# A hybrid encoder block on one core: the transfers that turn the feed-forward input spread over the projections, and a third of the weight sums moved to the last gates

## The chip, the cores and the metric

The kernel runs on one core of a Trainium2 chip. Its metric is the device time of one execution in microseconds (us). Three runs of the kernel before gave 865.10, 865.54 and 866.94 us, median 865.54. The profile is of one more execution, which took 866.11 us. Its trace covers a span of 864.3 us of that; the remaining 1.8 us lie around the span.

The engines have the profile's names: PE (TensorE, matrix products), DVE (VectorE), ACT (ScalarE), POOL (GpSimd), and SP (SyncE, which here only issues DMA transfers). POOL issues transfers too. Each engine works through its own instructions strictly in the order in which they stand. An instruction that waits for a semaphore holds up everything behind it on that engine.

## What is computed

The input is x of 512 rows by 1024 columns. Three token mixers (an mLSTM, a neighbourhood attention with a table of biases, a cross-attention into a memory) are merged by gates, projected, added to x, and followed by a feed-forward part and a normalization:

```python
h = rms_norm(x, mix_norm_g)
ml_q, ml_k, ml_v, ml_o, ml_gates, na_qkv, xa_q, merge_pre = split(h @ w_in)
g_ml, g_na, g_xa = split(sigmoid(merge_pre + b_merge_gate))
merged = g_ml * (y_ml @ w_br_ml) + g_na * (y_na @ w_br_na) + g_xa * (y_xa @ w_br_xa)
x = x + merged @ w_out
a, u = split(rms_norm(x, ffn_norm_g) @ w_ffn_up)          # 2816 columns each
x = x + (gelu(dwconv3(a, w_ffn_conv)) * u) @ w_ffn_down
return rms_norm(x, final_norm_g)
```

## The kernel before

**Layout and products.** Activations lie transposed, with channels on the 128 partitions and the 512 rows along the free axis, so x is eight tiles of 128x512. Each float32 product is made of three matmuls (`mm3`, L259 to L262): high part by high part, high part by low part, low part by high part. A *projection* (`proj`, L455) makes one tile of 128 output channels from eight input tiles, with 24 matmuls into one PSUM bank.

**Weights.** The weights are consumed in one fixed list of blocks (`BLOCKS`), each of 512 KB for a projection. SP loads a block into a tile `wr` (`emit_raw`, L206; three buffers, asked for three blocks ahead). It is then split in two halves: for each half ACT makes the high part `wh` (L242) and DVE the low part `wl` (L243, block minus high part). There are four buffers for high and four for low halves. In the code the split of a block stands one block ahead of the projection that uses it (`SPLIT_AHEAD`), but the instructions of each engine are put into their final order when the program is built, by a scheduler that may move them ahead of or behind their place in the code.

**Weight sums.** The down projection is computed from sums of quarters of its weight matrix, T1 to T4, held in DRAM. `sum_steps` (L163 to L174) makes them in 24 steps. Each step is a one-column copy on POOL (L169), which waits for the low half of a weight block and so sets the step's time, and behind it one transfer on POOL's own queue: a copy of a third of a quarter (L172) or the addition of another third to it (L174). The table `SUMS` (L64) says how many steps go to a projection of a kind: 0.5 is one step for every second projection. Before, 2 steps go to the `nak` projections, 6 to the first gates, 8 to the 8 output projections and 8 to the feed-forward projections `ua`.

**The stages around the change**, by the time in the profile's span:

- *Last gates* (about 383 to 436 us): eight gate projections of branch 2. Between them runs the end of the neighbourhood attention. Each of its steps loads a bias tile `nab` of 256 KB (`bias_tile`, L896, two buffers, on SP), and adds it to the scores on DVE (L914, two per step); ACT takes the exponentials (L919) and scales them (L922), and PE transposes the result (L928).
- *Output projections* (to about 510 us): eight projections `out` (loop at L1208), each followed by the addition of a residual tile that SP loads from `xT` (L1206, L1214) and a split of the new x2 into high and low parts.
- *Feed-forward, first half* (`hh` = 0, from about 510 us): the loop over f at L1344 takes two projections per step, `ua` and `uu`. On the `ua` bank follow, in a row: L518 (DVE, multiplies the bank into `pad`), L520 (ACT), L521 and L522 (DVE), which make the convolution, then L1375 (ACT), L1376 (DVE), L1377 (ACT) and L1378 (DVE), which make the gelu, and L1379 (POOL, a multiplication). On the `uu` bank: L1390 (DVE) multiplies it by the gelu, then come two halves of a split, L1322 (ACT) and L1323 (DVE), with a subtraction on POOL between them (L1393).
- From f = 1 to f = 8 each step also *turns* one tile of x2, since the final sum is wanted with rows on the partitions. `turned` (L557) does a transposition of 32x32 blocks on DVE (L559) and four transfers on SP (L561, one for each *band* of 32 partitions, 64 KB each in pieces of 128 bytes) to `c_d` in DRAM. At f = 9 `fetch` (L1237) reads `c_d` back with four transfers of 512 KB. `turn_keys` uses `turned` as well, much earlier in the program.

Of the kernel before, what the change touches and what calls it, by code (L numbers as in the profile page):

```python
# [11 lines left out]
F32 = mybir.dt.float32  # L12
# [5 lines left out]
P = 128  # L18
S = 512
D = 1024  # L20
KT = D // P
NT = S // P
# [38 lines left out]
NVEC = _o  # L61


SUMS = {"nak": 0.5, ("g", 0): 0.75, "out": 1.0, "ua": 0.75}  # L64
PRODUCTS = (("B11", "T3"), ("B21", "T1", "T2", "B22", "T4"))
QUARTERS = ("B11", "B12", "B21", "B22")

# [54 lines left out]
def hybrid_block(ctx, tc, xg, xT, memT, wflat, vecs, gbias, nabias, out):  # L122
    nc = tc.nc
    V, A, G, PE, SY = nc.vector, nc.scalar, nc.gpsimd, nc.tensor, nc.sync
# [5 lines left out]
    tp = ctx.enter_context(tc.tile_pool(name="tp", bufs=2))  # L130
    mmp = ctx.enter_context(tc.tile_pool(name="mmp", bufs=4, space=bass.MemoryType.PSUM))
    atp = ctx.enter_context(tc.tile_pool(name="atp", bufs=4, space=bass.MemoryType.PSUM))
    dp = ctx.enter_context(tc.tile_pool(name="dp", bufs=1, space=bass.MemoryType.DRAM))
# [3 lines left out]
    def nm(s):  # L137
        uid[0] += 1
        return f"{s}_{uid[0]}"

    def unit(dt=F32):
        return up.tile([P, UNIT], dt, tag="unit", name=nm("u"))
# [191 lines left out]
    for i in range(2):  # L334
        t = cp.tile([P, 514], F32, name=f"pad{i}")
# [119 lines left out]
    def proj(key, XHs, XLs, n=S, at={}, ps=None):  # L455

        ws = weights(key)
        if (key[0], key[1]) in SUMS or key[0] in SUMS:
            sum_step(SUMS.get(key[0]) or SUMS[key[:2]], ws)
        k0 = 0 if ps is None else 1  # L460
        if ps is None:
            ps = mmps()
        for k in range(k0, KT):
            mm3(ps[:, :n], ws[k][0], ws[k][1], XHs[k], XLs[k], k == 0, k == KT - 1)
            if k == 1:
                flush()
            if k in at:
                at[k]()
        return ps
# [60 lines left out]
    qT, kT = unit(), unit()  # L530
# [25 lines left out]

    def turned(x, src, dst, o=0):  # L557

        V.transpose(x, src)  # L559
        for a in range(4):  # L560
            SY.dma_start(dst[:, o + 32 * a:o + 32 * a + 32].rearrange("(b i) j -> i b j", i=32),  # L561
                         x[32 * a:32 * a + 32].rearrange("i (b j) -> i b j", j=32))

    kt_d = [dp.tile([S, P], F32, name=f"kt_d{f}") for f in range(4)]

    def turn_keys(f):

        with tc.issue_after(st["lo"]):
            turned(tp.tile([P, S], F32, tag="H", name=nm("kx"), bufs=4), kT[:, f * S:(f + 1) * S], kt_d[f])

    Gt = cp.tile([P, NT, 16], F32, name="Gt")
    va_u = unit()
# [3 lines left out]
    for c in range(3):  # L576
        n, nk = TMC[c], TMK[c]
# [142 lines left out]
    def ml_all():  # L720
# [18 lines left out]
        def keys(h):  # L739
# [4 lines left out]
            wva = u[:, :774].rearrange("p (d c e) -> p d c e", d=2, c=3)  # L744
            C = u[:, 774:1548].rearrange("p (d c e) -> p d c e", d=2, c=3)

# [47 lines left out]

        def values_J(h, J, E, ps, C, H, ss):
            js = slice(J * P, (J + 1) * P)
# [297 lines left out]
    for f in range(4):  # L1094
        ps = proj(("o", f), XH, XL)
        t = scr()
# [50 lines left out]
    for br in range(3):  # L1147
# [19 lines left out]
        for fp in range(4):  # L1167
# [9 lines left out]
            for i in range(2):  # L1177
                f = 2 * fp + i
# [18 lines left out]
    x2 = [x2u[f // 4][:, (f % 4) * S:(f % 4 + 1) * S] for f in range(KT)]  # L1197
# [2 lines left out]
    HL = [h2[k // 4 * 2 + 1][:, (k % 4) * S:(k % 4 + 1) * S] for k in range(KT)]  # L1200
    acc2 = cp.tile([P, S], F32, name="acc_2", tag="acc", bufs=1)
    xrs = {}

    def load_residual(f):
        xrs[f] = scr()
# [2 lines left out]
    for f in range(KT):  # L1208
        if f == 0:
            load_residual(0)  # L1210
        if f + 1 < KT:
            load_residual(f + 1)
        ps = proj(("out", f), GH, GL)
        V.tensor_tensor(x2[f], ps, xrs[f], op=ALU.add)  # L1214
        split_act(HH[f], HL[f], x2[f], vcol("ffn_g", f))
        if f == 0:
            A.activation(acc2, x2[f], AF.Square)
        else:
            sq = scr()
            A.activation(sq, x2[f], AF.Square)  # L1220
            V.scalar_tensor_tensor(acc2, acc2, EPS * D / P if f == 1 else 0.0, sq, op0=ALU.add, op1=ALU.add)


    C = [unit(), unit()]

    def cv(t, f):
        o = t % 2 * D + f * S
        return C[t // 2][:, o:o + S]

    c_d = dp.tile([S, D], F32, name="c_d")  # L1230

    def turn(f):

        turned(C[f // 4][:, (f % 4) * S:(f % 4 + 1) * S], x2[f], c_d, f * P)

    def fetch(t):
        SY.dma_start(C[t // 2][:, t % 2 * D:(t % 2 + 1) * D], c_d[t * P:(t + 1) * P, :])  # L1237
# [98 lines left out]
    for hh in range(2):  # L1336
        if hh == 0:
            a11, s3 = parts(), parts()
        else:
            ru = [unit() for _ in range(3)]  # L1340
            r1 = [ru[j // 4][:, j % 4 * S:(j % 4 + 1) * S] for j in range(HF)]
            a12, s1 = parts(), parts()
        for j in range(HF):
            f = HF * hh + j  # L1344
            if f == 0:
                wa, wu = weights(("ua", f)), weights(("uu", f))
                pa, pu = mmps(), mmps()
                for k in range(KT):
                    if k < KT - 1:
                        mm3(pa, wa[k][0], wa[k][1], HH[k], HL[k], k == 0, False)  # L1350
                for k in range(KT - 1):
                    mm3(pu, wu[k][0], wu[k][1], HH[k], HL[k], k == 0, False)
                k = KT - 1
                mm3(pa, wa[k][0], wa[k][1], HH[k], HL[k], False, True)
                rb2 = rstd_wide(square_sums(two_parts(acc2, S), S), S, "2")
                mm3(pu, wu[k][0], wu[k][1], HH[k], HL[k], False, True)
                pa1 = proj(("ua", 1), HH, HL)
                pu1 = proj(("uu", 1), HH, HL)
            else:
                pa = pa1 if f == 1 else proj(("ua", f), HH, HL)  # L1360
                if 1 <= f < KT + 1:
                    turn(f - 1)
                if f == KT + 1:
                    for t in range(NT):
                        fetch(t)
            cell = {}
            ve = V if j >= HF - 2 else G

            def conved(f=f, pa=pa, cell=cell):
                cell["c"] = conv(pa, rb2, "ffw", "ffb", f, FT)  # L1370

            def gelu(cell=cell, ve=ve):

                c, sq = cell["c"], scr()
                A.activation(sq, c, AF.Square)  # L1375
                V.scalar_tensor_tensor(sq, sq, GC, c, op0=ALU.add, op1=ALU.mult)  # L1376
                A.activation(sq, sq, AF.Tanh, scale=GK)  # L1377
                V.scalar_tensor_tensor(c, sq, 1.0, c, op0=ALU.add, op1=ALU.mult)  # L1378
                ve.tensor_tensor(c, c, rb2, op=ALU.mult)  # L1379

            if j < HF - 1:
                conved()
                gelu()
            if f > 0:
                pu = pu1 if f == 1 else proj(("uu", f), HH, HL)

            def gated(j=j, pu=pu, cell=cell, ve=ve):

                r, q, c = (r1 if hh else r0)[j], r0[j], cell["c"]
                V.scalar_tensor_tensor(r, pu, 0.5, c, op0=ALU.mult, op1=ALU.mult)  # L1390
                if hh == 0:
                    split_half(a11, j, r[:, one_])
                    ve.tensor_tensor(r[:, one_], r[:, two_], r[:, one_], op=ALU.subtract)  # L1393
                    late.append(lambda: split_half(s3, j, r[:, one_]))
                else:
                    split_half(a12, j, r[:, one_])
                    ve.tensor_tensor(q[:, two_], q[:, two_], r[:, two_], op=ALU.subtract)
                    late.append(lambda: split_half(s1, j, q[:, two_]))
                    ve.tensor_tensor(q[:, one_], q[:, one_], r[:, two_], op=ALU.subtract)
                    ve.tensor_tensor(r[:, one_], r[:, one_], q[:, one_], op=ALU.add)  # L1400

            if j < HF - 1:
                gated()
        if hh == 0:
            pa_, pd = [atps() for _ in range(2)], [mmps() for _ in range(2)]
            product("B11", a11, pa_, True, then={0: [conved], 1: [gelu], 2: [gated]})
            product("T3", s3, pd, True, then={1: [lambda: gather(pa_, 0, 0, ALU.add)]})
            late.append(lambda b=pd: (gather(b, 1, 0, ALU.subtract), gather(b, 1, 1, ALU.add)))
# [175 lines left out]
```

## Time and profile before

| quantity | value |
|---|---|
| runs: median (lowest to highest) | 865.54 us (865.10 to 866.94) |
| the profiled execution | 866.11 us |
| its span in the trace | 864.3 us |
| mean granted PE clock | 0.997 of full speed |
| DVE, ACT, POOL busy | 633.5, 476.1, 164.5 us |
| queue 1 (SP's transfers) | 107.66 MB, 38.7% of 16 DMA engines' time |
| queue 0 (POOL's transfers) | 29.39 MB, 14.0% |

The table is from the head of the profile's page. Busy time there is the time in which an engine has an instruction in work. For PE that includes waits inside its pipeline at half clock, so its share alone doesn't say that nothing is lost. The granted clock is the share of clock pulses that the throttle let through. The rows on PE itself are shown in the prediction.

### The profile page before, as it was taken

Reading aid. Unit: us, or ns where it says so; the run is one execution under the profiler, and the core shown is the slowest. Engines: PE = TensorE matmul, PEld = TensorE weight load, DVE = VectorE, ACT = ScalarE, POOL = GpSimd, SP = SyncE. Lnnn points to the kernel's source line nnn. Section 1 sums busy time; section 2 is a strip of 40 time slices with the busy share of each in tenths; the row PEclk is TensorE's granted clock in tenths of the full one; section 3 lists DMA queues with packets and bytes.
Section 4 is the critical chain, followed back from the end, with each engine's and each line's share of the span. In section 5 each row is a group of like instructions: output and inputs, shape, how many; then the busy total and the mean of one; then the engine's idle time right before and its main releaser. Section 6 shows DMA issues by size and latency. Waiting matters only on the chain.

```text
span 864.3 us, 12229 instructions
## 1 busy us (share of the span) xinstructions
PE 854.2 (99%) x4144; PEld 719.8 (83%) x4144; DVE 633.5 (73%) x1281; ACT 476.1 (55%) x1014; POOL 164.5 (19%) x279
## 2 busy tenths in 40 slices
PE   9999999999999999999999999989999999999996
PEld 7898889988888888888888888868888888888885
DVE  7696677775568758898767558776786777779786
ACT  7364447644546658888644445444454444446763
POOL 0101100001013593700002102322200333320001
PEclk9999999999999999999999999999999999999999
DMA  8326743533485655543236965846866323226563
GB/s 278 101 71 177 220 144 123 184 121 135 158 195 131 204 148 152 156 137 110 98 110 189 323 193 138 215 138 171 258 200 207 98 98 97 89 83 209 187 205 144
DMA packets 70256, 138.24 MB, mean 160 GB/s; under 512 B 31848, under 2 KB 39016, under 8 KB 68592
## 3 DMA queue, kind: packets, MB, share of 16 engines
q1 hardware_dynamic: 60416, 107.66, 38.7%
q0 software_dynamic: 9344, 29.39, 14.0%
q8 instruction: 33, 0.54, 0.3%
q10 hardware_dynamic: 432, 0.39, 0.1%
q14 instruction: 31, 0.25, 0.1%
HBM read 130.06 MB, written 30.43 MB: 186 GB/s over the span
## 4 chain that ended last, share of the span: by engine, by line
PE 91%; DVE 3%; issue 2%; ACT 1%; POOL 1%; DMA 0%; POOLq 0%; DVEq 0%; ACTq 0%
PE mm L260 23%; PE mm L262 23%; PE mm L261 23%; PE at L1273 2%; PE at L1275 2%; PE at L1274 2%; PE at L261 2%; PE at L260 2%; PE at L262 2%; PE mm L1273 1%; PE mm L1275 1%; PE mm L1274 1%; PE at L947 1%; PE at L800 1%; PE at L928 1%
## 5 line engine op out<-in xcount | busy, mean ns | idle before, releaser
L260 PE MATMUL mm<-u,wh 128*128 128x512 f32 (+1 forms) x907 | 354.0, 390 | 1.6 <-ACT wh L242 1.6
L262 PE MATMUL mm<-u,wl 128*128 128x512 f32 (+1 forms) x907 | 351.1, 387 | 1.0 <-DVE wl L243 0.9
L261 PE MATMUL mm<-u,wh 128*128 128x512 f32 (+1 forms) x907 | 350.2, 386 | 0.0
L242 ACT ACTIVATE wh<-wr 128x512 fp32r<-128x512 f32 (+2 forms) x328 | 202.2, 624 | 164.1 <-PE mm L261 103.1
L243 DVE TENSOR_TENSOR wl<-wr,wh 128x512 fp32r<-128x512 f32 (+2 forms) x330 | 233.2, 711 | 65.2 <-ACT wh L242 60.0
L262 PEld LDWEIGHTS mm<-u,wl 128*128 128x128 f32 x907 | 170.7, 188 | 37.0 <-DVE wl L243 2.3
L260 PEld LDWEIGHTS mm<-u,wh 128*128 128x128 f32 x907 | 171.0, 189 | 34.6 <-ACT wh L242 2.0
L261 PEld LDWEIGHTS mm<-u,wh 128*128 128x128 f32 x907 | 170.8, 188 | 33.0
L616 POOL DMA_DIRECT2D u<-nav_d x128 | 62.8, 531 | 27.7 <-PE at L947 15.7
L1379 POOL TENSOR_TENSOR s<-s,rb 128x512 f32<-128x512 f32 x18 | 29.3, 1626 | 112.7 <-DVE s L1378 105.7
L169 POOL COPY y<-wl 128x1 f32<-128x1 f32 x24 | 6.7, 279 | 226.9 <-DVE wl L243 226.9
L1322 ACT ACTIVATE u<-r 128x256 fp32r<-128x256 f32 x44 | 17.7, 414 | 39.6 <-DVE r L1390 23.5
L1273 PE MATMUL at<-wh,u 128*128 128x512 f32 x100 | 39.1, 391 | 0.0
L1275 PE MATMUL at<-wh,u 128*128 128x512 f32 x100 | 38.9, 389 | 0.0
L1274 PE MATMUL at<-wl,u 128*128 128x512 f32 x100 | 38.9, 389 | 0.0
L520 ACT ACTIVATE s<-pad,vec 128x512 f32<-128x512 f32 x30 | 24.3, 810 | 20.6 <-DVE pad L518 20.6
L1323 DVE TENSOR_TENSOR u<-r,u 128x256 fp32r<-128x256 f32 x44 | 20.4, 473 | 10.7 <-ACT u L1322 10.7
L521 DVE SCALAR_TENSOR_TENSOR s<-pad,vec,s 128x512 f32<-128x512 f32 x30 | 22.5, 750 | 5.9 <-ACT s L520 5.8
L1375 ACT ACTIVATE s<-s 128x512 f32<-128x512 f32 x22 | 13.9, 632 | 21.3 <-DVE s L522 21.2
L1378 DVE SCALAR_TENSOR_TENSOR s<-s,s 128x512 f32<-128x512 f32 x22 | 15.2, 690 | 10.7 <-ACT s L1377 10.5
L522 DVE SCALAR_TENSOR_TENSOR s<-pad,vec,s 128x512 f32<-128x512 f32 x30 | 22.5, 748 | 0.7
L1275 PEld LDWEIGHTS at<-wh,u 128*128 128x128 f32 x100 | 18.8, 188 | 3.9
(332 smaller groups left out, 1237.5 us busy)
## 6 DMA issues: line engine op xcount, KB each, us to landing
wr<-wflat SPq DMA_DIRECT2D x140, 512.0 KB, 3.8
wr<-wsum_T SPq DMA_DIRECT2D x20, 512.0 KB, 3.7
wsum_T<-wflat POOLq DMA_DIRECT2D x8, 1024.0 KB, 9.9
wsum_T<-wflat POOLq DMA_DIRECT2D x6, 768.0 KB, 7.5
nab<-nabias SPq DMA_DIRECT2D x16, 256.0 KB, 2.6
u<-nav_d POOLq DMA_DIRECT2D x128, 32.0 KB, 3.1
s<-xT SPq DMA_DIRECT2D x15, 256.0 KB, 4.9
nav_d<-nv POOLq DMA_DIRECT2D x8, 256.0 KB, 2.9
```

Source lines behind the costliest of these rows:

```text
L242: st["hi"] = A.activation(h[:, u:v], src, AF.Copy).ins
L243: st["lo"] = V.tensor_tensor(l[:, u:v], src, h[:, u:v].bitcast(F32), op=ALU.subtract).ins
L260: PE.matmul(ps, lh, rh, start=start, stop=False)
L261: PE.matmul(ps, lh, rl, start=False, stop=False)
L262: st["mm"] = PE.matmul(ps, ll, rh, start=False, stop=stop).ins
L520: A.activation(t1, pad[:, 0:512], AF.Identity, scale=vcol(w, i), bias=vcol(b, i))
L521: V.scalar_tensor_tensor(t1, pad[:, 1:513], vcol(w, n + i), t1, op0=ALU.mult, op1=ALU.add)
L616: G.dma_start(vw[r * 32:(r + 1) * 32, i * 256:(i + 1) * 256], nav_v[hf, r, CW[b]:CW[b] + 32, hp * 256:(hp + 1) * 256])
L1273: PE.matmul(bank, ah[:, ts], w[0], start=start, stop=False, skip_group_check=True)
L1274: PE.matmul(bank, ah[:, ts], w[1], start=False, stop=False, skip_group_check=True)
L1275: st["mm"] = PE.matmul(bank, al[:, ts], w[0], start=False, stop=True, skip_group_check=True).ins
L1379: ve.tensor_tensor(c, c, rb2, op=ALU.mult)
```

## The change

The table of sums gets an entry for the last gates, one step for each of the eight gate projections, and halves the rate of the output projections (4 steps instead of 8) and lowers that of the `ua` projections (4 steps instead of 8). The 24 steps and their order stay.

`turned` no longer issues its transfers itself but returns four functions, one per band, of which the first also does the transposition. They go to a list `turns` as soon as a tile of x2 exists, in the loop of the output projections. `turn(n)` takes the next n of them: one after each output projection with f over 1, one after each `ua` (two at f = 7 and 8), two after each `uu`. The fetches are made at f = 9 and 10, one after each of the four projections. `turn_keys` calls its four functions at once, as before. The two tiles `C` and the DRAM tensor `c_d` are allocated ahead of the output loop.

```diff
-SUMS = {"nak": 0.5, ("g", 0): 0.75, "out": 1.0, "ua": 0.75}
+SUMS = {"nak": 0.5, ("g", 0): 0.75, ("g", 2): 1.0, "out": 0.5, "ua": 0.5}
...
     def turned(x, src, dst, o=0):

-        V.transpose(x, src)
-        for a in range(4):
+        def band(a):
+            if a == 0:
+                V.transpose(x, src)
             SY.dma_start(dst[:, o + 32 * a:o + 32 * a + 32].rearrange("(b i) j -> i b j", i=32),
                          x[32 * a:32 * a + 32].rearrange("i (b j) -> i b j", j=32))
+        return [lambda a=a: band(a) for a in range(4)]
...
+    C = [unit(), unit()]
+    c_d = dp.tile([S, D], F32, name="c_d")
+    turns = []
+
+    def turn(n):
+        for _ in range(n):
+            if turns:
+                turns.pop(0)()
...
+        if f > 1:
+            turn(1)
+        turns += turned(C[f // 4][:, (f % 4) * S:(f % 4 + 1) * S], x2[f], c_d, f * P)
...
                 pa = pa1 if f == 1 else proj(("ua", f), HH, HL)
-                if 1 <= f < KT + 1:
-                    turn(f - 1)
-                if f == KT + 1:
-                    for t in range(NT):
-                        fetch(t)
+                turn(1 + (f in (7, 8)))
+                if f in (KT + 1, KT + 2):
+                    fetch(2 * (f - KT - 1))
...
                 pu = pu1 if f == 1 else proj(("uu", f), HH, HL)
+                turn(2)
+                if f in (KT + 1, KT + 2):
+                    fetch(2 * (f - KT - 1) + 1)
```

PE's own order doesn't change. The change moves instructions on the other engines, and the rows below show what stands there before and after. A tile's number differs between the two programs; equal numbers within one listing are one tile.

The first place is ACT in the feed-forward loop around the conv of f = 4, in the kernel before. The rows begin with the conv and gelu of f = 3; `wh_5934` and `wh_5938` are the two halves of the block `uu` of f = 4, `wh_5990` and `wh_5994` those of `ua` of f = 5.

```order
L520 ACTIVATE s_5883<-pad_153,vec 128x512
L1375 ACTIVATE s_5887<-s_5883 128x512
L1377 ACTIVATE s_5887<-s_5887 128x512
L242 ACTIVATE wh_5934<-wr_5837 128x512
L242 ACTIVATE wh_5938<-wr_5837 128x512
L1322 ACTIVATE u_5544<-r_5535 128x256
L1322 ACTIVATE u_5547<-r_5535 128x256
L520 ACTIVATE s_5978<-pad_150,vec 128x512
L242 ACTIVATE wh_5990<-wr_5893 128x512
L242 ACTIVATE wh_5994<-wr_5893 128x512
```

The same place in the changed kernel, where L520 of before keeps its number, L1375, L1377 and L1322 are L1380, L1382 and L1329, and the blocks `uu` of f = 4 and `ua` of f = 5 are `wr_5854` and `wr_5904`.

```order
L520 ACTIVATE s_5894<-pad_153,vec 128x512
L1329 ACTIVATE u_5567<-r_5554 128x256
L242 ACTIVATE wh_5947<-wr_5854 128x512
L1380 ACTIVATE s_5898<-s_5894 128x512
L1382 ACTIVATE s_5898<-s_5898 128x512
L242 ACTIVATE wh_5951<-wr_5854 128x512
L1329 ACTIVATE u_5564<-r_5555 128x256
L242 ACTIVATE wh_5999<-wr_5904 128x512
L1329 ACTIVATE u_5567<-r_5555 128x256
L242 ACTIVATE wh_6003<-wr_5904 128x512
L520 ACTIVATE s_5987<-pad_150,vec 128x512
```

Before, both halves of the next `ua` block stood behind the conv of the tile in work (L520); now both stand ahead of it.

The second place is DVE at the conv of f = 2, where the transpositions (L559) stand before:

```order
L1323 TENSOR_TENSOR u_5544<-r_5532,u_5544 128x256
L559 STREAM_TRANSPOSE u_5529<-u_5156 128x512
L1390 SCALAR_TENSOR_TENSOR r_5533<-mm_5680,s_5726 128x512
L1323 TENSOR_TENSOR u_5547<-r_5532,u_5547 128x256
L559 STREAM_TRANSPOSE u_5529<-u_5156 128x512
L1323 TENSOR_TENSOR u_5544<-r_5533,u_5544 128x256
L518 TENSOR_TENSOR pad_150<-mm_5753,rb_5626 128x512
L243 TENSOR_TENSOR wl_5801<-wr_5670,wh_5800 128x512
```

And in the changed kernel, where L1390 and L1323 are L1398 and L1330, and `wl_5816` is the half that was `wl_5801`:

```order
L1330 TENSOR_TENSOR u_5564<-r_5552,u_5564 128x256
L243 TENSOR_TENSOR wl_5816<-wr_5690,wh_5815 128x512
L1398 SCALAR_TENSOR_TENSOR r_5553<-mm_5700,s_5742 128x512
L1330 TENSOR_TENSOR u_5567<-r_5552,u_5567 128x256
L518 TENSOR_TENSOR pad_150<-mm_5772,rb_5646 128x512
L1330 TENSOR_TENSOR u_5564<-r_5553,u_5564 128x256
L243 TENSOR_TENSOR wl_5820<-wr_5690,wh_5819 128x512
```

Two transpositions have left this place, one of the halves moved ahead of the conv, and one L1330 fell behind it. Of the eight transpositions four now stand in the output projections, each some way behind the addition of its residual, and four between the convs of f = 2 and f = 3 (before, two stood ahead of the conv of f = 2, two between f = 2 and 3, and four between f = 4 and 5).

The third place is POOL's queue, from the last of the attention's value loads (L616, in the changed kernel L620), which belong to the last gates. Before, the next step of the sums is that of the first output projection:

```order
L616 DMA u_4322<-nav_d 32x256 x32
L169 COPY y_5177<-wl_5099 128x1
L172 DMA wsum_T_2_80<-wflat 16x12288
L169 COPY y_5221<-wl_5170 128x1
L174 DMA wsum_T_0_78<-wflat 128x2048
```

And in the changed kernel it is that of the first of the last gates, eight steps in eight projections, of which five are shown:

```order
L620 DMA u_4322<-nav_d 32x256 x32
L169 COPY y_4487<-wl_4382 128x1
L172 DMA wsum_T_2_80<-wflat 16x12288
L169 COPY y_4569<-wl_4480 128x1
L174 DMA wsum_T_0_78<-wflat 128x2048
L169 COPY y_4651<-wl_4562 128x1
L174 DMA wsum_T_1_79<-wflat 128x2048
L169 COPY y_4733<-wl_4644 128x1
L174 DMA wsum_T_2_80<-wflat 96x2048
L169 COPY y_4813<-wl_4726 128x1
L172 DMA wsum_T_0_81<-wsum_T_0_78 16x16384
```

The same transfers in the same order now follow the low halves of the gates' blocks. On SP the first sixteen bands now stand two or so behind each weight load, from the load for the output projection f = 5 to that for `ua` of f = 2, with the last residual loads between them; before, the first eight stood together behind the load for `ua` of f = 4.

More of the change, by code (lines that the diff above doesn't have):

```diff
@@ L568, in turn_keys @@
         with tc.issue_after(st["lo"]):
-            turned(tp.tile([P, S], F32, tag="H", name=nm("kx"), bufs=4), kT[:, f * S:(f + 1) * S], kt_d[f])
+            for band in turned(tp.tile([P, S], F32, tag="H", name=nm("kx"), bufs=4), kT[:, f * S:(f + 1) * S], kt_d[f]):
+                band()
     Gt = cp.tile([P, NT, 16], F32, name="Gt")
@@ L1221, in hybrid_block @@
             V.scalar_tensor_tensor(acc2, acc2, EPS * D / P if f == 1 else 0.0, sq, op0=ALU.add, op1=ALU.add)
-    C = [unit(), unit()]
+        if f > 1:
+            turn(1)
+        turns += turned(C[f // 4][:, (f % 4) * S:(f % 4 + 1) * S], x2[f], c_d, f * P)
     def cv(t, f):
@@ L1228, in cv @@
         return C[t // 2][:, o:o + S]
-    c_d = dp.tile([S, D], F32, name="c_d")
-    def turn(f):
-        turned(C[f // 4][:, (f % 4) * S:(f % 4 + 1) * S], x2[f], c_d, f * P)
     def fetch(t):
```

## The prediction, made before the changed kernel was run

> **What bounds the kernel now.** I read the head of the page first, then the waits of PE, then busy time by windows, and last the instructions around the one place where PE loses time. The head gives busy time by engine:
>
> ```profile
> PE 854.2 (99%) x4144; PEld 719.8 (83%) x4144; DVE 633.5 (73%) x1281; ACT 476.1 (55%) x1014; POOL 164.5 (19%) x279
> ```
>
> PE is busy for 99% of the span, the others for 73% at most. The waits of PE alone (engine, line, what it waited for, us in total, times, longest):
>
> ```profile
> PE mm L260 <- ACT wh L242: 1.6, 1, 1.6
> PE mm L262 <- DVE wl L243: 0.9, 1, 0.9
> ```
>
> There are two, each once: the high half of a weight block from ACT, then its low half from DVE. Windows of 50 us (busy time and instructions of PE, PEld, DVE, ACT and POOL, the granted clock, DMA share, GB/s) say the same:
>
> ```profile
> 550.00:600.00 50.00, 47.46 (x202) 38.23 (x201) 34.84 (x56) 20.99 (x39) 12.64 (x15) 0.97 0.55 161
> 600.00:650.00 50.00, 50.00 (x222) 41.42 (x221) 38.99 (x62) 25.97 (x47) 5.79 (x6) 1.00 0.77 222
> ```
>
> So PE's matmuls bound the kernel. Their number and order don't change. The change can gain only what PE loses at this place, and it can cost only by making PE wait somewhere new. What was lost stands in PE's timeline (start, duration, line):
>
> ```profile
> 539.97 0.39 PE L261 MATMUL mm<-u,wh 128*128 128x512 f32 x1
> 540.48 0.50 PE L262 MATMUL mm<-u,wl 128*128 128x512 f32 x1
> ...
> 559.69 0.39 PE L261 MATMUL mm<-u,wh 128*128 128x512 f32 x1
> ...
> 561.96 0.39 PE L262 MATMUL mm<-u,wl 128*128 128x512 f32 x1
> 563.96 0.50 PE L260 MATMUL mm<-u,wh 128*128 128x512 f32 x1 [1.62 <-ACT wh L242]
> ...
> 565.62 0.80 PE L262 MATMUL mm<-u,wl 128*128 128x512 f32 x1 [0.93 <-DVE wl L243]
> ...
> 568.66 0.40 PE L260 MATMUL mm<-u,wh 128*128 128x512 f32 x1
> ```
>
> Starts are what count, since matmuls overlap. From 559.69 to 561.96 lie ten steps in 2.27 us, 0.227 each; a projection of 24 takes 5.44. From 561.96 to 568.66 lie ten steps too, in 6.70 us. So **4.43 us** are lost: 1.77 in the first wait (2.00 less one step), 1.21 in the two steps to 565.62 (1.66 less 0.45), and 1.45 in the seven steps after it (3.04 less 1.59), which ran slowly with no wait. The clock granted in that stretch shows why:
>
> ```profile
> 565.00:575.00 10.00, 9.38 (x35) 7.67 (x36) 7.56 (x14) 4.17 (x8) 2.35 (x2) 0.83 0.28 73
> ```
>
> At 0.83 in 10 us, 1.7 us of full clock are missing. At 540 us one step took 0.51 instead of 0.23, another **0.28 us**, for a low half on DVE.
>
> The Trainium skill ("TensorE: Matmul & The Clock Gate", section "What's actually happening") says that the clock is halved after at least one idle window of about 3.4 us. No idle time here is that long, yet the clock fell: the trace disagrees, at least on how full such a window must be. By the page's rule the slow steps had some other cause and would stay when the waits go: 865.54 − 1.77 − 1.21 − 0.28 = 862.3 us. By the rows they set in within the hole and end 2.7 us after its last wait, so I count them to it.
>
> **Why there is a hole.** Not a transfer. The block needed at 563.96 is `ua` of f = 5. SP issued its load at 546.8, and it landed 8.9 us later:
>
> ```profile
> L206 SPq DMA_DIRECT2D wr<-wflat x1: 2293/2293/2293, 546.8 to 546.8; - x1
> ...
> DMA to landing us min/median/max: 8.9/8.9/8.9
> ```
>
> so it lay there at 555.7. Its split started at 563.29. In between stands a chain of instructions that wait for one another across three engines. On POOL, on DVE and on ACT:
>
> ```profile
> 556.48 1.67 POOL L1379 TENSOR_TENSOR s<-s,rb 128x512 f32<-128x512 f32 x1 [5.59 <-DVE s L1378]
> ```
> ```profile
> 558.62 0.68 DVE L1390 SCALAR_TENSOR_TENSOR r<-mm,s 128x512 f32<-128x512 f32 x1
> ...
> 561.85 0.69 DVE L518 TENSOR_TENSOR pad<-mm,rb 128x512 f32<-128x512 f32 x1
> ...
> 564.88 1.28 DVE L243 TENSOR_TENSOR wl<-wr,wh 128x512 fp32r<-128x512 f32 x2
> ```
> ```profile
> 562.58 0.81 ACT L520 ACTIVATE s<-pad,vec 128x512 f32<-128x512 f32 x1 [1.10 <-DVE pad L518]
> 563.29 1.14 ACT L242 ACTIVATE wh<-wr 128x512 fp32r<-128x512 f32 x2
> ```
>
> The split of f = 5 stands behind the conv of f = 4 on ACT (L520), and that waits for L518 on DVE, which waits its turn behind the gelu and the split of f = 3. ACT sat idle ahead of L520 with a loaded block at hand. So it is **the order** that costs, together with a conv that had fallen behind.
>
> **What the change does there.** The listing of ACT above shows both L242 of that block ahead of L520 now, with no part of the conv of f = 4 in front of them. That is the pattern which the kernel before has itself from f = 8 on. There the conv starts at
>
> ```profile
> 598.13 0.69 DVE L243 TENSOR_TENSOR wl<-wr,wh 128x512 fp32r<-128x512 f32 x1
> 598.74 0.69 DVE L518 TENSOR_TENSOR pad<-mm,rb 128x512 f32<-128x512 f32 x1
> ```
>
> with the next low half done before it, and the window from 600 to 650 above has PE at 50.00 of 50. So the order can feed PE, if the chain isn't later than there. My chain by hand, with the steps between starts as these rows have them (0.73 from L518 to L520, 2.14 from L1379 to L1390, 3.23 from L1390 to L518): two transpositions and one L1323 no longer stand ahead of the conv of f = 2, which starts 0.9 us earlier; the conv of f = 3 starts near 548.9, that of f = 4 near 559.7 instead of 561.85. The halves of f = 5 don't wait for it and stand ready over 2 us before PE wants them (an estimate). So the first hole goes whole: −4.43.
>
> The half that was late at 540 is the low half of `ua` f = 3. It moves ahead of L1390 and of the conv of f = 2: −0.28.
>
> The transpositions and bands only move. By the rows of their lines (duration min/median/max in ns, first and last start) and of the additions that read the result:
>
> ```profile
> L559 DVE STREAM_TRANSPOSE u<-u x8: 669/703/708, 535.3 to 574.4; 128x512 f32<-128x512 f32 x8
> ```
> ```profile
> L561 SPq DMA_DIRECT2D c_d<-u x32: 302/504/3858, 536.0 to 604.9; - x32
> ```
> ```profile
> L1281 DVE TENSOR_TENSOR u<-u,at x10: 678/680/682, 651.1 to 847.0; 128x512 f32<-128x512 f32 x10
> ```
>
> Four transpositions go to the output projections, 4 x 0.70 = 2.8 us of DVE in eight projections of 5.44 us. Four stand between the convs of f = 2 and f = 3, where two stood: +1.4 us, which fall beside L1379, for whose 2.14 us L1390 waits anyway. Their result is read back by f = 10, about 620 us, and used at 651.1, so no band can be late. SP's part is 16 bands x 0.5 = 8 us in the output projections, next to the weight loads. Four of the eight sums go from there. I take nothing for either. If the cover is gone, a late half costs as at f = 5 before, 1 to 4.4 us.
>
> The sums put eight transfers into the last gates. Landing times of weight loads there and in the output projections, which had eight sums before, and of the bias tiles in the last gates (min/median/max):
>
> ```profile
> DMA to landing us min/median/max: 3.2/3.3/4.3
> ```
> ```profile
> DMA to landing us min/median/max: 4.7/11.3/12.7
> ```
> ```profile
> DMA to landing us min/median/max: 2.5/2.6/2.6
> ```
>
> So a load takes up to 3.4 times as long beside sums. Yet PE had no wait in the output projections at 12.7 us. The bias tiles have the lead that these rows give:
>
> ```profile
> 384.67 0.33 SPq L896 DMA_DIRECT2D nab<-nabias  x1
> ```
> ```profile
> 396.94 0.41 DVE L914 CUSTOM_DVE_ANT_0 s<-at,nab 128x256 f32<-128x256 f32 x1
> ```
> ```profile
> 407.06 0.91 ACT L922 ACTIVATE s<-s,y 128x256 f32<-128x256 f32 x2
> ```
> ```profile
> 410.80 0.60 PE L928 MATMUL at<-ident,s 128*128 128x128 f32 x4
> ```
>
> 12.3 us from issue to use, and 2.8 us more between the end of ACT's scaling and PE's transposition. PE waits only from a landing of about **15.1 us** on. The bounds for a bias tile are 2.6 us (unchanged) and 12.7 (the slowest load beside sums, of twice the size). I take 2.6 x 3.4 = 8.9: no cost.
>
> **The sum.** −4.43 − 0.28 = −4.71. Against the profiled execution: 866.11 − 4.71 = 861.40. The runs shown have a median of 865.54, 0.57 lower, so 860.83: **860.8 us**.
>
> **The rivals.**
>
> *A part of the hole stays or comes back nearby.* For it: at 540 us a half was already late by 0.28, so the margins at f = 2 to 5 are thin, the four transpositions are bunched there, and one L243 beside L1379 in a chain as above costs DVE time. Against it: ready over 2 us ahead. One wait like the second one, 1.21, up to one with slow steps, 1.21 + 1.45 = 2.66, remains: 862.0 to 863.5, with both waits 864. Of the same kind: the waits go, but the slow steps stay for a reason of their own, 1.45: 862.3.
>
> *The hole isn't due to the order.* If ACT's idle time ahead of L520 only stood in for a limit that the trace doesn't show, the gain is nothing: 865.5. Against it: the block had landed 7.6 us before its split.
>
> *Slower: the last gates run out of DMA.* If bias tiles beside the sums land later than 15.1 us, DVE's L914 waits; behind it in DVE's order stand the low halves of the gates' weights and the gates' own work, and PE waits at L928. Three steps can meet it. A landing of 18 us costs 2.9 and, as at 563 us, about 1.45 of slow steps, 4.4 in all; two or three of these give 8.8 to 13.1 less the 4.7: 869.6 to 873.9. Against it: the largest landing shown is 12.7.
>
> On this the Trainium skill ("DMA: Bandwidth & Descriptors", section "Queues, rings and completion order") says that each DMA engine takes turns between queues, packet by packet. By that a load beside one other queue would take about twice as long, 5.2 us, an estimate from the page; the row of the output projections, 11.3 against 3.3, is worse than that. Both stay below 15.1.
>
> **How the numbers follow.** Forecast (860.3 to 861.9) 68%, as the order at fault is gone word for word and the new one is seen at work from f = 8 on. Part of the hole 16% (862 to 864.5), of which 3% for slow steps that stay. No gain 7% (around 865.5). Slower 9%. Low end: the lowest run, 865.10, less 4.71 and a little, 859.9. High end 864.5, which leaves out the last two cases, 16%. What a measurement of this kernel can tell from no change is about 0.2%, 1.7 us: faster is below 863.8, slower above 867.3. Faster holds the forecast and most of the partial case less the chance that other runs scatter, as 866.94 does: 0.77. Same 0.14, slower 0.09.
>
> **What would show it.** PE's waits in the changed profile name neither L242 nor L243, and the window from 550 to 600 shows 50.00 and clock 1.00. L518 of f = 4 starts below 560.5 and stands behind the low half of f = 5. In the last gates weight loads land in some 9 to 13 us, bias tiles below 13, with PE at 10.00 of 10 in each window. A wait of PE before 450 us, or a low clock at f = 2 to 6, would make the prediction wrong.

## The result, and the profile after

Six runs of the changed kernel have a median of **861.36 us** (861.08 to 861.50), against 865.98 us for six runs of the kernel before (865.10 to 867.13). The ratio is 0.9945, with a 95% interval of 0.9933 to 0.9958: 4.6 us less. The profiled execution took 861.32 us, with a span of 859.5 us, 4.8 less than before. The runs of the kernel before scatter with their mean granted clock: of the 57 made beside the experiments below, the 28 at 0.998 or 0.999 took 864.88 to 866.02 us, the 21 at 0.997 took 866.09 to 867.44, and the 8 at 0.994 took 867.21 to 867.80, while the eleven runs of the changed kernel, at 0.997 to 0.999, took 860.56 to 861.50.

The waits of PE in the changed kernel (engine, line, what it waited for, us in total, times, longest) hold neither of the two rows that stood there before, only the one at the start of the program, which before had too:

```profile
PE at L289 <- PEq L1585: 0.8, 1, 0.8
```

The windows of 50 us (busy time of PE, PEld, DVE, ACT and POOL with instructions, clock, DMA share, GB/s) answer to those of before. The one from 550 to 600 has 20 matmuls more and the full clock:

```profile
550.00:600.00 50.00, 50.00 (x222) 41.42 (x221) 37.54 (x56) 23.20 (x42) 12.81 (x14) 1.00 0.79 208
600.00:650.00 50.00, 50.00 (x223) 41.39 (x222) 38.63 (x61) 25.74 (x45) 4.09 (x4) 1.00 0.45 141
```

At the place of the hole ACT and DVE now do this (timelines of ACT, then DVE; `ua` of f = 5 is split by the L242 at 558.43 and 560.16 and the L243 at 559.08 and 561.23; L518 and L520 are the conv of f = 4):

```profile
558.11 0.42 ACT L1329 ACTIVATE u<-r 128x256 fp32r<-128x256 f32 x1 [2.71 <-DVE r L1398]
558.43 0.62 ACT L242 ACTIVATE wh<-wr 128x512 fp32r<-128x512 f32 x1
559.83 0.42 ACT L1329 ACTIVATE u<-r 128x256 fp32r<-128x256 f32 x1 [0.79 <-POOL r L1401]
560.16 0.61 ACT L242 ACTIVATE wh<-wr 128x512 fp32r<-128x512 f32 x1
561.35 0.82 ACT L520 ACTIVATE s<-pad,vec 128x512 f32<-128x512 f32 x1 [0.57 <-DVE pad L518]
```
```profile
559.08 1.27 DVE L243 TENSOR_TENSOR wl<-wr,wh 128x512 fp32r<-128x512 f32 x1
560.28 0.42 DVE L1330 TENSOR_TENSOR u<-r,u 128x256 fp32r<-128x256 f32 x1
560.63 0.68 DVE L518 TENSOR_TENSOR pad<-mm,rb 128x512 f32<-128x512 f32 x1
561.23 0.68 DVE L243 TENSOR_TENSOR wl<-wr,wh 128x512 fp32r<-128x512 f32 x1
```

The first high half stands ready at 559.05 instead of 563.91. In the last gates and then in the output projections the weight loads land in (min/median/max):

```profile
DMA to landing us min/median/max: 4.8/5.6/9.0
```
```profile
DMA to landing us min/median/max: 3.2/5.2/8.0
```

and the bias tiles of the last gates in

```profile
DMA to landing us min/median/max: 4.5/7.5/8.5
```

So the sums do slow the loads where they went, from 3.3 to 5.6 us and from 2.6 to 7.5, and free them where they left, from 11.3 to 5.2, and PE waits in neither place.

### The profile page after: what moved, and what is told of

It is laid out like the page before. It is cut to its first block, busy times and chain, and to the rows that moved or that the text cites. A ratio compares the mean times of both kernels' runs of the same rounds, so it can differ in the third digit from the quotient of the medians.

```text
span 859.5 us, 12230 instructions
## 1 busy us (share of the span) xinstructions
PE 851.7 (99%) x4144; PEld 718.9 (84%) x4144; DVE 636.6 (74%) x1281; ACT 476.8 (55%) x1014; POOL 164.2 (19%) x279
## 4 chain that ended last, share of the span: by engine, by line
PE 97%; DVE 1%; DMA 1%; POOL 0%; issue 0%; ACT 0%; POOLq 0%; DVEq 0%
PE mm L260 25%; PE mm L262 25%; PE mm L261 25%; PE at L1280 2%; PE at L1282 2%; PE at L1281 2%; PE at L261 2%; PE at L260 2%; PE at L262 2%; PE mm L1280 1%; PE mm L1282 1%; PE mm L1281 1%; PE at L951 1%; PE at L804 1%; PE at L932 1%; PE at L769 1%
## 5 line engine op out<-in xcount | busy, mean ns | idle before, releaser
L242 ACT ACTIVATE wh<-wr 128x512 fp32r<-128x512 f32 (+2 forms) x328 | 203.0, 625 | 171.9 <-PE mm L261 109.4
L243 DVE TENSOR_TENSOR wl<-wr,wh 128x512 fp32r<-128x512 f32 (+2 forms) x330 | 235.8, 718 | 67.0 <-ACT wh L242 61.4
L620 POOL DMA_DIRECT2D u<-nav_d x128 | 62.6, 527 | 28.2 <-PE at L951 14.6
L1329 ACT ACTIVATE u<-r 128x256 fp32r<-128x256 f32 x44 | 17.7, 414 | 36.3 <-DVE r L1398 23.1
L520 ACT ACTIVATE s<-pad,vec 128x512 f32<-128x512 f32 x30 | 24.3, 811 | 19.3 <-DVE pad L518 19.3
L1380 ACT ACTIVATE s<-s 128x512 f32<-128x512 f32 x22 | 13.9, 632 | 20.1 <-DVE s L522 19.9
L1330 DVE TENSOR_TENSOR u<-r,u 128x256 fp32r<-128x256 f32 x44 | 20.4, 474 | 5.7 <-ACT u L1329 5.7
```

What stands on the lines that cost most here:

```text
L242: st["hi"] = A.activation(h[:, u:v], src, AF.Copy).ins
L243: st["lo"] = V.tensor_tensor(l[:, u:v], src, h[:, u:v].bitcast(F32), op=ALU.subtract).ins
L520: A.activation(t1, pad[:, 0:512], AF.Identity, scale=vcol(w, i), bias=vcol(b, i))
L620: G.dma_start(vw[r * 32:(r + 1) * 32, i * 256:(i + 1) * 256], nav_v[hf, r, CW[b]:CW[b] + 32, hp * 256:(hp + 1) * 256])
```

## The experiments

The theory: PE lost its 4.7 us by the order on ACT and DVE, where the split of a block stood behind a conv. The rivals are the sums' traffic, a conv that comes too late whatever the order, and the early start of the turning. Each ratio is against runs of the kernel before on the same chip.

### One half of the change at a time

The kernel before with the new table of sums, and the changed kernel with the old one. In the traces ACT, DVE and SP have the order of before in the first and that of the changed kernel in the second; only POOL's differs.

```diff
-SUMS = {"nak": 0.5, ("g", 0): 0.75, "out": 1.0, "ua": 0.75}
+SUMS = {"nak": 0.5, ("g", 0): 0.75, ("g", 2): 1.0, "out": 0.5, "ua": 0.5}
```

> The kernel before with the new table of sums only. The transfers that turn x2 stay as they were. Theory 'order': ACT, DVE and SP keep the order of before, so the hole at 562 us stays; 865.5 to 866.2 us, PE waits once on a high and once on a low half. Rival 'sums': the sums' transfers and marks beside the feed-forward projections made the chain late, and moving them cures it; 861.2 to 861.6.

> The changed kernel with the old table of sums. Theory 'order': ACT and DVE have the order of the changed kernel, so there is no hole; 861.1 to 861.7, no wait of PE. Rival 'sums': the hole is back, 865.5 to 866.2.

The sums alone: 865.99 us, ratio 0.9997 (0.9987 to 1.0007). The turning alone: 860.97, ratio 0.9939 (0.9924 to 0.9954), 0.1 us below what the theory gave and with no wait of PE. With the sums alone PE has the same two waits as before, to the tenth:

```profile
PE mm L260 <- ACT wh L242: 1.6, 1, 1.6
PE mm L262 <- DVE wl L243: 0.9, 1, 0.9
```

The whole gain is the turning's. The rival of the sums falls.

### The order alone, and the lateness alone

In the kernel before, the split of one block, `ua` of f = 5, is put ahead of the conv of f = 4. In the changed kernel the same split is put back behind that conv. The first keeps the transpositions ahead of the conv where they were, the second keeps them away.

```diff
-            if j < HF - 1:
+            if f == 4:
+                emit_split(st["split"])
+                st["split"] += 1
+                with tc.issue_after(st["hi"]), tc.issue_after(st["lo"]):
+                    conved()
+                    gelu()
+            elif j < HF - 1:
```

```diff
-            emit_split(st["split"])
+            if BLOCKS[st["split"]][0] == ("ua", 5):
+                with tc.issue_after(st["conv"]):
+                    emit_split(st["split"])
+            else:
+                emit_split(st["split"])
...
-        A.activation(t1, pad[:, 0:512], AF.Identity, scale=vcol(w, i), bias=vcol(b, i))
+        st["conv"] = A.activation(t1, pad[:, 0:512], AF.Identity, scale=vcol(w, i), bias=vcol(b, i)).ins
```

> The kernel before, with the split of one block, ua of f = 5, put ahead of the conv of f = 4; the transpositions stay. Theory 'order': the hole of 4.4 us goes and the 0.3 us at 540 stay; 861.4 to 862.2. Rival 'lateness' (the conv of f = 4 comes too late whatever stands behind it): the wait passes to the next block, uu of f = 5 or ua of f = 6; 863 to 866.

> The changed kernel, with the split of ua of f = 5 put behind the conv's ACT instruction of f = 4, as it stood before; the transpositions stay where the change put them. Theory 'order': PE waits again, some 0.9 us for the high half and 0.5 us for the low one, with or without slow steps; 862.6 to 864.4. Rival 'lateness': the conv is 1.2 us earlier than before, so nothing is lost; 861.1 to 861.7.

The split ahead, in the kernel before: 862.76 us, ratio 0.9962 (0.9947 to 0.9977). That is 0.6 us above what the theory gave, and below the rival's range. Both waits at 562 us are gone. A new loss stands further on, at the block of `ua` of f = 8 (PE's timeline):

```profile
595.30 0.39 PE L262 MATMUL mm<-u,wl 128*128 128x512 f32 x1
595.94 0.50 PE L260 MATMUL mm<-u,wh 128*128 128x512 f32 x1 [0.25 <-ACT wh L242]
596.28 0.40 PE L261 MATMUL mm<-u,wh 128*128 128x512 f32 x1
596.67 0.50 PE L262 MATMUL mm<-u,wl 128*128 128x512 f32 x1
```

That is 0.64 − 0.23 and 0.39 − 0.23, some 0.6 us, and the 0.3 at 540 stay. With the smaller late steps beside these and at 557 and 563, PE loses 1.8 us in the feed-forward projections; the spans differ by as much (861.3 against 859.5 of the changed kernel). At the new place the split stands on ACT behind L1322, which waits 1.31 us for POOL. The edit had also moved the four last transpositions from ahead of the conv of f = 5 to behind it; whether that made the new loss wasn't tried. The conv of f = 4 even starts later than before here, at 563.6, and at that place PE loses 0.14 us in one step and 0.11 in the next. So the conv's lateness by itself makes next to nothing of the hole.

The split behind, in the changed kernel: 862.83 us, ratio 0.9957 (0.9943 to 0.9971), within what the theory gave. PE waits again at the old place:

```profile
561.31 0.39 PE L266 MATMUL mm<-u,wl 128*128 128x512 f32 x1
562.71 0.50 PE L264 MATMUL mm<-u,wh 128*128 128x512 f32 x1 [1.02 <-ACT wh L242]
563.05 0.40 PE L265 MATMUL mm<-u,wh 128*128 128x512 f32 x1
563.58 0.50 PE L266 MATMUL mm<-u,wl 128*128 128x512 f32 x1
```

1.17 for the high half and 0.30 for the low one, 1.5 us against 4.4 before, with no slow steps behind it. The order alone brings back a hole in a kernel whose conv is early, and the earlier conv makes that hole smaller. Each of the two cures alone is worth some 3.5 us (866.36 for the kernel before on this chip, less 862.76 and 862.83). They overlap, and only together do they give the whole, 5.4 us on this chip by the 860.97 of the turning alone.

### Where the turning begins, and in what lots

First, single bands as in the change, but none in the output projections. Second, four bands of a tile at once as before, but from the output projections on.

```diff
-        if f > 1:
-            turn(1)
...
-                turn(1 + (f in (7, 8)))
+                turn(2)
```

```diff
         if f > 1:
-            turn(1)
+            turn(4)
...
-                turn(1 + (f in (7, 8)))
+                turn(4)
...
-                turn(2)
```

> The changed kernel, except that the turning begins only with the up-projections (two bands after each ua and each uu from f = 1 to 8, none in the output projections). Two transpositions stand ahead of the conv of f = 2 again, as before, but both halves of ua of f = 5 stand ahead of the conv of f = 4. Theory 'order': the hole of 4.4 us is gone, the 0.3 to 0.4 us at 540 are back; 861.3 to 862.0. Rival 'early start' (the gain is from turning half of x2 in the output projections): 863 to 866.

> The changed kernel, except that a tile's four bands go out together again, one tile after each output projection from f = 2 and one after ua of f = 1 and 2. The splits stand ahead of the convs everywhere. Theory 'order': no hole; 861.0 to 861.7. Rival 'spreading' (single bands are what lets the weight loads through): waits of PE on weights, 862.5 to 866.

Single bands from the up-projections on: **863.84 us**, ratio 0.9971 (0.9960 to 0.9981). That is outside what the theory gave, and in the range of the rival. The big hole is gone, but there are small ones, for low halves that DVE makes late with transpositions and splits of its own around them:

```profile
573.65 0.39 PE L261 MATMUL mm<-u,wh 128*128 128x512 f32 x1
574.35 0.50 PE L262 MATMUL mm<-u,wl 128*128 128x512 f32 x1 [0.30 <-DVE wl L243]
```
```profile
596.05 0.39 PE L261 MATMUL mm<-u,wh 128*128 128x512 f32 x1
596.82 0.50 PE L262 MATMUL mm<-u,wl 128*128 128x512 f32 x1 [0.38 <-DVE wl L243]
```

0.47 and 0.54 us, with 0.3 at 540. With the smaller late steps beside these and at 557 and 563, PE loses 2.3 us, and the spans differ by 2.4 (861.9 against 859.5). Half of the turning in the output projections is thus a part of the gain, of some 2.4 us. I had counted only the place at 540 for it. My reading is that it takes DVE work out of a loop in which the halves are made with little to spare. That fits the place at 574, which has two transpositions around the late half. At 597 it is only argued: the last transposition stands at 577.3, and the half that is late there took 1.27 us on DVE where others take 0.69.

Whole tiles from the output projections on: **864.62 us**, ratio 0.9981 (0.9972 to 0.9991; one run of 950 us, outside everything else, is not in the interval). That too is outside what the theory gave, and in the range of the rival. All transpositions are early here (the last at 508.0), yet a hole of the old kind stands at another place, the convs of f = 0 and 1. Waits of PE, and ACT there:

```profile
PE mm L262 <- DVE wl L243: 1.3, 1, 1.3
PE mm L260 <- ACT wh L242: 1.0, 2, 0.8
```
```profile
523.51 0.81 ACT L520 ACTIVATE s<-pad,vec 128x512 f32<-128x512 f32 x1 [3.01 <-DVE pad L518]
524.23 1.13 ACT L242 ACTIVATE wh<-wr 128x512 fp32r<-128x512 f32 x2
```

The split that PE waited for stands right behind L520, as at 563 us before, while ACT sat idle for 3.0 us ahead of it. The block had been issued at 505.7 and landed

```profile
DMA to landing us min/median/max: 3.8/3.8/3.8
```

later, at 509.5, 14 us before PE wanted it. So the rival's mechanism, weight loads held up by the bands, isn't what costs here; it is the order again, at a place that the expectation had left out, since I had read the order at f = 2 to 8 and not at f = 0. In lots of four the bands stand between the weight loads on SP, and in both kernels with such lots the builder put a split behind a conv at a place where on the chip the block was there long before. That the lots are what makes it plan so wasn't tried by itself and stays open.

### How many sums the last gates bear

The rival on the slower side. Sixteen sums there, and then twelve (with a loop in place of the `if` in `sum_step`, so that a projection can take two):

```diff
-SUMS = {"nak": 0.5, ("g", 0): 0.75, ("g", 2): 1.0, "out": 0.5, "ua": 0.5}
+SUMS = {"nak": 0.5, ("g", 0): 0.75, ("g", 2): 2.0}
```

```diff
-SUMS = {"nak": 0.5, ("g", 0): 0.75, ("g", 2): 1.0, "out": 0.5, "ua": 0.5}
+SUMS = {"nak": 0.5, ("g", 0): 0.75, ("g", 2): 1.5, "out": 0.5}
```

> The changed kernel with sixteen sums, two per projection, in the last gates, and none later. Theory of the prediction (PE waits there only when a bias tile takes over 15.1 us to land): landings of bias tiles of 8 to 13 us, no wait; 861.0 to 861.7. Rival 'last gates run out of DMA': landings over 15.1 us and waits of PE between 385 and 440; 865 to 874.

> The changed kernel with twelve sums in the last gates (one and two per projection in turn), four in the output projections, none later. With sixteen a bias tile that took 17.1 us to land cost PE 0.9 us, so the point is near 16.2 us. Theory 'point': longest landing of a bias tile between 8.5 (eight sums) and 22 (sixteen), near 15, so no wait of PE there or one under 1 us; 861.0 to 862.5. Rival 'saturation' (with more than eight sums the DMA engines fall behind for good, so that weight blocks come late too): 864 to 870.

Sixteen: **876.21 us**, ratio 1.0116 (1.0100 to 1.0133), slower than before the change and than either range. Bias tiles took up to 22.0 us to land and weight blocks up to 27.2. Against the changed kernel PE loses some 9 us in the last gates and 7 more up to 487 us, mostly in waits for splits of activations (L266 on ACT, 1.73 us at most) and in the slow steps after them. Twelve: **866.11 us**, ratio 1.0001 (0.9992 to 1.0010): four sums more give back the whole gain. That is outside what the theory gave and in the range of the rival, but not by its mechanism: weight loads did take up to 20.7 us, yet no wait of PE names one. With twelve, one bias tile, issued at 397.6, lands 19.8 us later; DVE waits for it, and PE for DVE (landing, DVE, PE, and the window with the clock 0.83):

```profile
DMA to landing us min/median/max: 19.8/19.8/19.8
```
```profile
417.49 0.42 DVE L918 CUSTOM_DVE_ANT_0 s<-at,nab 128x256 f32<-128x256 f32 x1 [6.90 <-DMA nab<-nabias]
```
```profile
416.92 0.28 PE L914 MATMUL at<-KS,QZ 128*128 128x256 f32 x1
419.65 0.56 PE L951 MATMUL at<-w,u 128*128 128x256 f32 x2 [2.46 <-DVE w L940]
420.86 0.56 PE L951 MATMUL at<-w,u 128*128 128x256 f32 x2 [0.64 <-DVE w L940]
```
```profile
415.00:425.00 10.00, 6.90 (x28) 5.61 (x27) 6.34 (x22) 5.07 (x15) 1.80 (x4) 0.83 0.45 154
```

DVE was held for 6.9 us, but PE's waits are 3.1; the rest was slack. 19.8 − 3.1 leaves a point near 16.7 us, against 15.1 in the prediction and 16.2 in the expectation. The place at which PE waits is one that I hadn't named: the product behind the chain of transposed scores (L951), not the transposition (L932). The longest landing goes from 8.5 us with eight sums to 19.8 with twelve and 22.0 with sixteen, so it doesn't grow in proportion; the middle that I had expected, near 15, is wrong.

### Is the sums' move worth anything?

> The changed kernel itself again, beside the next one on one chip. 860.9 to 861.5.

> The changed kernel with the old table of sums again. If the sums' move is worth nothing in itself, the same time as the changed kernel within 0.4 us; a rival by which the sums' transfers cost something in the last gates has it faster by more than that.

> The changed kernel with the old table of sums a third time, for the spread of its runs. Two of its ten runs so far lay over 862 us and the others within 860.3 to 861.4, while eleven runs of the changed kernel lay within 860.5 to 861.5. If the late weight block in the output projections is a matter of chance with the old table, some runs lie over 862 again; if those two were a disturbance of another kind, none.

On one chip the changed kernel has 861.14 us (860.56 to 861.47) and the one with the old sums 861.09: no difference in the median. But one of these runs, the profiled one, took 863.47, and another 862.30. Its profile has a wait that no profile of the changed kernel has, at a weight load issued at 499.2:

```profile
DMA to landing us min/median/max: 13.0/13.0/13.0
```
```profile
512.31 1.15 ACT L242 ACTIVATE wh<-wr 128x512 fp32r<-128x512 f32 x2 [6.40 <-DMA wr<-wflat]
```
```profile
511.90 0.39 PE L262 MATMUL mm<-u,wl 128*128 128x512 f32 x1
513.00 0.50 PE L260 MATMUL mm<-u,wh 128*128 128x512 f32 x1 [0.70 <-ACT wh L242]
```

Here it is the transfer. With eight sums and sixteen bands in the output projections a load can take 13.0 us, and then PE loses 0.9 us in that step and 1.3 with the three after it, of the 2.4 us by which this run is late. In the changed kernel the longest is 8.0 (rows above). In the two other profiles with the old sums it is 12.2 and 12.6, with no wait of PE. The third set of runs, though, had none over 861.45 (median 861.09). So two of fifteen runs with the old sums are late and none of eleven with the new ones: the mechanism is seen in one profile, how often it strikes isn't settled.

### Waits of a known size

> The changed kernel with three added waits in the output projections: after f = 1, 3 and 5 PE transposes a scratch tile that DVE has made from the finished bank in one, two and three steps, and only then goes on; nothing uses the result. Waits of about 0.9, 2.1 and 3.5 us, 6.5 us in all. Theory 'a part of a window is enough': the second and the third are followed by slow steps, some 1.5 us each; 869 to 871. Rival, by the clock rule of a window of about 3.4 us that must be idle: only the third; 867 to 869.

```diff
...
+    HOLES = {1: 0, 3: 1, 5: 2}
+
+    def hole(ps, n):
+        t = scr()
+        V.tensor_tensor(t, ps, rb, op=ALU.mult)
+        for _ in range(n):
+            V.tensor_tensor(t, t, rb, op=ALU.mult)
+        return PE.transpose(atps()[:, :P], t[:, :P], ident).ins
...
+        if f in HOLES:
+            st["hole"] = hole(ps, HOLES[f])
```

The matmuls of the next projection are held until that transposition (edit not shown). One run: 869.84 us. PE's timeline at the second and the third added wait:

```profile
485.63 0.39 PE L262 MATMUL mm<-u,wl 128*128 128x512 f32 x1
488.09 0.30 PE L1228 MATMUL at<-ident,s 128*128 128x128 f32 x1 [2.07 <-DVE s L1227]
488.15 0.48 PE L260 MATMUL mm<-u,wh 128*128 128x512 f32 x1
488.47 0.39 PE L261 MATMUL mm<-u,wh 128*128 128x512 f32 x1
```
```profile
502.58 0.30 PE L1228 MATMUL at<-ident,s 128*128 128x128 f32 x1 [3.28 <-DVE s L1227]
...
503.44 0.63 PE L260 MATMUL mm<-u,wh 128*128 128x512 f32 x1
503.87 0.63 PE L261 MATMUL mm<-u,wh 128*128 128x512 f32 x1
...
506.83 0.39 PE L262 MATMUL mm<-u,wl 128*128 128x512 f32 x1
```

After a wait of 2.07 us the steps are normal at once. After 3.28 us steps of 0.43 follow from 503.44 to 506.43. My theory had expected slow steps after both and falls for the middle one; the total (869.84, expected 869 to 871) would not have told that.

## Why the prediction was right

**The bound and the hole.** PE's order was the same, only PE's losses could come back, and all of them did: 4.71 us were summed, the spans differ by 4.8 and the medians by 4.62. That the numbers agree to 0.1 us is in part luck. The sum left out some 0.4 us of smaller late steps (0.13 and 0.10 at 557, and single steps beside those that were counted), so that PE's last matmul comes 5.1 us earlier, and the stretch behind it became 0.4 longer. And the sum is that of one execution, while the runs of before differ among themselves by almost 3 us.

**The slow steps.** They were counted to the hole, and went with it: the window from 550 to 600 has the clock at 1.00. The case in which they stay for a reason of their own falls. But 1.45 us is what they cost in the profiled execution. The groups of runs in the section on the result suggest that not every execution of the kernel before has them, and that some have more: the runs at the higher clocks lie some 4 us above the changed kernel, those at 0.994 over 6. The two traces with this hole, those of the kernel before and of the sums alone, both have the slow steps, so this isn't shown.

**The cause.** "It is the order that costs, together with a conv that had fallen behind" is what the pair of order and lateness showed, with a size for each that the prediction didn't have: some 3.5 us for the cure of either alone. The sentence on the order "gone word for word" carried the forecast; the same look at f = 0 and 1 would have been needed for a kernel such as the one with whole tiles.

**The chain by hand.** The convs were expected near 548.9 and 559.7. They started at 548.92 and 560.63: the step from f = 3 to f = 4 took 11.7 us and not 10.8, so that "below 560.5" was missed by 0.1. It did no harm, since the halves of f = 5 don't wait for it. The conv of f = 2 started at 538.54, 0.5 us earlier than before and not 0.9, so the match at f = 3 is partly luck. "L518 of f = 4 stands behind the low half of f = 5" holds for the first low half only; the second, at 561.23, stands behind it. The first high half was ready 2.5 us ahead of PE and the first low one, by the row at 559.08, 1.6 us, where the prediction said over 2 for both.

**The transpositions and bands at no cost.** No cost was right in this kernel. "Two more between f = 2 and 3 fall beside L1379" held. What was under-rated is the gain in turning half of the tiles ahead of the loop, some 2.4 us by the run that doesn't. And the fetches weren't at 620 us but at 581.7, which changes nothing.

**The sums.** In the last gates 8.9 us were taken for a bias tile and 7.5 (at most 8.5) measured. For weight loads there I had named 9 to 13 and measured 4.8 to 9.0. The slower rival's mechanism is real, its point was placed to 1.6 us, and it lay closer than the 9% suggest: half as many sums again decide it. Its price, the landing less 15.1 and 1.45 for slow steps, gives some 6.2 us for the tile of 19.8 us with twelve sums. The spans differ by 4.8 (864.3 against 859.5); most of the difference is the misplaced point. For the four sums taken from the output projections the prediction took nothing; on the median that is right, but beside the bands they can make a load late, which it didn't name.

## What to carry to other kernels

When the engine that bounds waits once in a long loop, look at what its supplier did just before: an idle supplier, with its input long landed, behind an instruction that waits for something else, is an order to change, not a transfer to speed up. Moving unrelated work (here transfers that nobody waits for) can change such an order in a built program, so compare the order of every engine at every turn of the loop, the first ones too. A stage that bears eight background transfers at no cost can lose the whole gain with twelve: work out the landing from which somebody waits, and keep well away from it.

## What the runs showed of the hardware

The clock fell in places where PE's idle time was shorter than the window of the clock rule. Lost time in one place and what came after, by the start times of matmuls in one execution each: 2.2 us in one wait, normal steps; 1.0 and 1.5 us with two matmuls between (whole tiles), normal; 1.8 and 1.2 us with two matmuls between (the kernel before), slow steps; 2.6 and 0.9 us (twelve sums), slow; 3.4 us in one wait, slow. So a little work in between didn't protect. These executions change over between 2.5 and 3.0 us lost within some 4 us, but that isn't shown to be a fixed point: the runs of the kernel before fall in groups by clock, as if one and the same hole were followed by slow steps in some runs and not in others. The Trainium skill ("TensorE: Matmul & The Clock Gate", section "What's actually happening") has at least one idle window of about 3.4 us; these executions needed less idle time than that.

The slow stretches of these profiles had one length or twice it, whatever the hole. The granted clock is 0.50 for 3.4 us in the kernel before (565.1 to 568.5), after the third added wait (503.4 to 506.8) and with twelve sums (421.4 to 424.8), and for 6.8 us at two places with sixteen (429.2 to 436.0 and 480.4 to 487.2).

The landing of loads beside other transfers is far from even: 8.5, 19.8 and 22.0 us at most for the same bias tiles with eight, twelve and sixteen sums, at a DMA share of about 1.0 in all three by 405 us.
